# Four bias products on 32 rows each: one expert block of a streaming encoder on one Trainium2 core

## The chip, the cores and the metric

The kernel runs on one core of one Trainium2 chip. The time is device microseconds (us) of one execution, and lower is better. The engines are named as in the profile: PE is TensorE's matmuls and PEld its weight loads, DVE is VectorE, ACT is ScalarE, POOL is GpSimd, and SP is the engine that issues most of the transfers.

## The reference, cut to what matters

The block normalises its input, runs attention and a linear recurrence, projects, normalises again, and then sends each of 512 tokens through 4 of 32 experts. Only the expert part and its biases bear on this change:

```python
def expert_block(args):
    xb, e = args
    hb = xb @ w_up[e] + b_up[e]          # (128, 1024) @ (1024, 2048) + (2048,)
    glu, lin = jnp.split(hb, 2, axis=-1)
    ...
    return act @ w_down[e] + b_down[e]   # (128, 1024) @ (1024, 1024) + (1024,)
```

Everything is float32. `b_up` has 32 rows (experts) of 2048 columns.

## The kernel before

The kernel has three stretches: the mixer with the output projection, the routing, and the loop over the 32 experts. Each expert has one slot of 128 tokens. Its weights come from HBM in twelve chunks of 1 MB: eight of the up projection (128 rows by 2048 columns) and four of the down projection. Line 74 issues these loads on SP's queue whenever one of ten raw tiles (`w_raw`) is free. Each chunk is split into a high and a low part: line 87 rounds it on ACT (`w_hi_t`), line 89 subtracts on DVE (`w_lo_t`). A raw tile is free again once line 89 has read it. Every product is then three matmuls (lines 409 to 411): high by high, low by high, high by low.

The expert loop is written out in a fixed order by hand. For expert e it begins the up projection (`up_begin`), runs eight chunks of it with the transposes of the neighbouring experts in between, and then the four chunks of the down projection of expert e-1. On TensorE the last matmul of a down projection is thus followed by the bias products of the next expert, and these by its first chunk.

The bias of the up projection is added by matmul. `bias` is a tile of 128 rows by 2048 columns in bfloat16: rows 0 to 31 hold the first bfloat16 part of all 32 experts' biases, rows 32 to 63 the second part, rows 64 to 95 the third, and rows 96 to 127 zero. The stationary operand is one column of `erow_b`, broadcast to 128 columns; it is one in the three rows of expert e. Four such matmuls (line 414), one for each 512 columns, write the four PSUM tiles `ps_up_t` that the chunks then add to:

```python
    def bias_mm(self, ps, sel, j):
        self.nc.tensor.matmul(ps, sel, self.bias[:, 512 * j:512 * j + 512], start=True, stop=False)
```

Nearest to this in form is line 368 (`meta`), which runs once in four experts in the same loop: sixteen matmuls that each use 32 of the array's columns, with weights and results of 32 columns.

`prepare_up` (lines 321 to 336) fills `bias` once. It runs where the attention ends: its tiles lie in memory that the attention gives back. The bias is loaded in four pieces on ACT's queue, three casts on ACT and two subtractions on DVE form the parts, and twelve transfers on ACT's queue move each part to its rows. Around it TensorE works on the last projections of the mixer (lines 938 to 940, tile `pj`); line 1542 on ACT and line 1543 on DVE empty its two PSUM tiles. Then come the first chunks of the output weight (`w_raw` from `in_w_o`), split by lines 87 and 89. In this stretch the order on each engine comes from the compiler's scheduler, which goes by estimated times; from the normalisation behind the output projection on, the order is written by hand.

`erow` and `erow_b` are formed in `Consts` at the start. The overflow loop (line 687) serves experts with more tokens than a slot holds; in this run its body isn't entered.

Of the kernel before, what the change touches and what calls it, by code (L numbers as in the profile page):

```python
# [8 lines left out]
F32 = mybir.dt.float32  # L9
F32R = mybir.dt.float32r  # L10
BF = mybir.dt.bfloat16
I32 = mybir.dt.int32
AF = mybir.ActivationFunctionType
ALU = mybir.AluOpType
AX = mybir.AxisListType
# [6 lines left out]
NE = 32  # L22
# [9 lines left out]
BIG = 4096.0  # L32
# [10 lines left out]
class Stream:  # L43


    def __init__(self, tc):
        self.nc = tc.nc
        self.free = deque()
        self.split_ahead = 2
        self.queue = self.nc.sync  # L50
        self.src = []
        self.raws, self.parts = {}, {}
        self.loaded = self.split = 0
# [67 lines left out]
class Consts:  # L121
    def __init__(self, nc, pool, tmp):
        self.mhalf = pool.tile([128, 4], F32, name="mhalf")
        nc.gpsimd.memset(self.mhalf, -0.5)
        nc.scalar.copy(tmp.tile([128, 4], F32, name="act_table"), self.mhalf)
        jp = tmp.tile([128, 128], I32, name="jp")
        nc.gpsimd.iota(jp, pattern=[[1, 128]], base=0, channel_multiplier=-1)
        self.ident = pool.tile([128, 128], F32, name="ident")
        nc.vector.tensor_scalar(self.ident, jp, 0.0, None, op0=ALU.is_equal)
        self.before = pool.tile([128, 128], BF, name="before")  # L130
        nc.vector.tensor_scalar(self.before, jp, 0.0, None, op0=ALU.is_gt)
        self.ones = pool.tile([128, 128], BF, name="ones")
        nc.vector.memset(self.ones, 1.0)

        self.base = pool.tile([128, 1], F32, name="base")
        for b in range(NB):
            nc.gpsimd.memset(self.base[SLB * b:SLB * b + SLB, :], BIG + 128.0 * b)
        self.slots = pool.tile([128, 128], F32, name="slots")
        nc.gpsimd.iota(self.slots, pattern=[[1, 128]], base=-int(BIG), channel_multiplier=0,
                       allow_small_or_imprecise_dtypes=True)  # L140
        self.pcol = pool.tile([128, 1], F32, name="pcol")
        nc.gpsimd.iota(self.pcol, pattern=[[0, 1]], base=0, channel_multiplier=1,
                       allow_small_or_imprecise_dtypes=True)
        self.ecol = pool.tile([128, NE], F32, name="ecol")
        nc.gpsimd.iota(self.ecol, pattern=[[1, NE]], base=0, channel_multiplier=0,
                       allow_small_or_imprecise_dtypes=True)
        self.erow = pool.tile([128, NE], F32, name="erow")
        t = tmp.tile([128, NE], F32, name="sel_t")
        nc.vector.tensor_scalar(self.erow, jp[:, :NE], 0.0, None, op0=ALU.is_equal)
        for r in (1, 2):  # L150
            nc.vector.tensor_scalar(t, jp[:, :NE], -float(r * NE), None, op0=ALU.is_equal)
            nc.vector.tensor_add(self.erow, self.erow, t)
        self.erow_b = pool.tile([128, NE], BF, name="erow_b")
        nc.vector.tensor_copy(self.erow_b, self.erow)


class Moe:
# [162 lines left out]

    def prepare_up(self, tmp):

        nc = self.nc
        nc.gpsimd.memset(self.bias[96:128], 0.0)

        bq = tmp.tile([128, 512], F32, name="prep_b")
        for q in range(4):
            nc.scalar.dma_start(bq[32 * q:32 * q + 32], self.a["b_up"][0][:, 512 * q:512 * q + 512])
        for r in range(3):
            pt = tmp.tile([128, 512], BF, name=f"prep_p{r}")  # L330
            nc.scalar.copy(pt, bq)
            if r < 2:
                nc.vector.tensor_sub(bq, bq, pt)
            for q in range(4):
                nc.scalar.dma_start(self.bias[32 * r:32 * r + 32, 512 * q:512 * q + 512],
                                    pt[32 * q:32 * q + 32, :])

    def open(self, ctx, h1, h1_pool):
        tc, nc = self.tc, self.nc
# [70 lines left out]
        mm(ps, xh, wl, start=False, stop=False)  # L410
        mm(ps, xl, wh, start=False, stop=stop)  # L411

    def bias_mm(self, ps, sel, j):
        self.nc.tensor.matmul(ps, sel, self.bias[:, 512 * j:512 * j + 512], start=True, stop=False)

    def up_begin(self, sel):
        ps = [self.ps_up.tile([128, 512], F32, name="ps_up_t") for _ in range(4)]
        for j in range(4):
            self.bias_mm(ps[j], sel, j)
        return ps  # L420

    def up_chunk(self, ps, x, w, k):
# [149 lines left out]
            steps[step[0]](int(step[1]))  # L572

    def sel_of(self, e):
        return self.c.erow_b[:, e:e + 1].to_broadcast([128, 128])

    def experts(self, out):
        st = self.st
# [104 lines left out]
    def overflow(self, out):  # L683

        tc, nc, a, st = self.tc, self.nc, self.a, self.st
        n = nc.values_load(self.n_i[0:1, 0:1], min_val=0, max_val=3 * NE)
        with tc.For_i(0, n, 1) as i:
            ti = self.xp.tile([1, 2], I32, name="ov_i")
            nc.sync.dma_start(ti, self.tab_i[bass.ds(i, 1), :])
            tf = self.xp.tile([128, 2], F32, name="ov_f")  # L690
            row = self.tab_f[bass.ds(i, 1), :]
            nc.sync.dma_start(tf, row.to_broadcast([128, 2]))
            e = nc.values_load(ti[0:1, 0:1], engines=[mybir.EngineType.SP], min_val=0, max_val=NE - 1)
            em = self.xp.tile([128, NE], F32, name="ov_em")
            nc.vector.tensor_scalar(em, self.c.ecol, tf[:, 0:1], None, op0=ALU.is_equal)
            shift = self.xp.tile([128, 1], F32, name="ov_shift")
            nc.vector.tensor_scalar(shift, tf[:, 1:2], -float(SLB), None, op0=ALU.mult)
            pos = self.xp.tile([128, NB], F32, name="ov_pos")
            vals = self.xp.tile([128, NB, 5], BF, name="ov_vals")
            t = self.xp.tile([128, NE, 5], F32, name="ov_t", bufs=1)  # L700
            t3 = self.xp.tile([128, 5], F32, name="ov_t3")
            for b in range(NB):
                nc.vector.tensor_mul(t[:, :, 0], self.posm[:, b, :], em)
                nc.vector.tensor_reduce(pos[:, b:b + 1], t[:, :, 0], axis=AX.X, op=ALU.add)
                nc.vector.tensor_mul(t, self.vals[:, b], em[:, :, None].to_broadcast([128, NE, 5]))
                nc.vector.tensor_reduce(t3, t.rearrange("p e s -> p s e"), axis=AX.X, op=ALU.add)
                nc.vector.tensor_copy(vals[:, b, :], t3)
            nc.vector.tensor_scalar(pos, pos, shift, None, op0=ALU.add)
            self.onehot(pos[:, :, None], 1)
            drain(self.meta(1, lambda b, _: vals[:, b, :]))  # L710
            idx, gate = self.idx[-1], self.gate[-1]
            self.fetch(0, idx)
            drain(self.x_T(0))
            et = self.xp.tile([128, NE], F32, name="ov_et")
            nc.vector.tensor_mul(et, self.c.erow, em)
            sc = self.xp.tile([128, 1], F32, name="ov_sc")
            nc.vector.tensor_reduce(sc, et, axis=AX.X, op=ALU.add)
            sel_t = self.xp.tile([128, 1], BF, name="ov_sel")
            nc.vector.tensor_copy(sel_t, sc)
            sel = sel_t.to_broadcast([128, 128])  # L720
            wu = a["w_up"][0][bass.ds(e, 1)].rearrange("o k n -> (o k) n")
            wd = a["w_down"][0][bass.ds(e, 1)].rearrange("o k n -> (o k) n")

            def chunk(src):
                c = st.add(*src)
                return st.get(c)
            ps = self.up_begin(sel)
            for k in range(8):
                self.up_chunk(ps, self.x[0], chunk(self.up_src(wu, k)), k)
            for h in range(2):  # L730
                self.act0(ps, h)
                self.act1(ps, h)
                self.act2(h)
                drain(self.act_T(h))
            ps = self.dn_begin()
            for k in range(4):
                w = chunk(self.dn_src(wd, k))
                for kk in range(2):
                    self.dn_half(ps, w, k, kk)
            self.slots_T(idx)  # L740
            self.finish_on_chip(ps, gate, out)
# [140 lines left out]
def drain(g):  # L882
    for _ in g:
        pass
# [849 lines left out]
```

## Time and profile before

| | |
|---|---|
| median of 3 runs | 1526.08 us (1525.84 to 1527.07) |
| the profiled execution's own time | 1526.0 us |
| its span on the core | 1524.2 us |
| PE busy | 1463.3 us, 96% of the span |
| PEld busy | 1208.1 us, 79% |
| DVE busy | 1325.1 us, 87% |
| ACT busy | 1074.7 us, 71% |
| POOL busy | 263.8 us, 17% |
| HBM traffic | 310 GB/s over the span |

Busy shares are averages over stretches with different limits. Matmuls are pipelined: one that is listed with 0.39 us may start 0.23 us after the one before, so the distance between starts, and not the listed length, is what it costs. The span starts at 0 in all rows below.

### The profile page before, as it was taken

How to read it: one execution, taken by the hardware profiler on the slowest of the kernel's cores; microseconds unless marked ns; L12 is line 12 of the kernel's file. 1: busy time of each engine (PE TensorE's matmuls, PEld its weight loads, DVE VectorE, ACT ScalarE, POOL GpSimd, SP SyncE). 2: the span in 40 equal slices, each digit the busy share in tenths (PEclk: the TensorE clock that was granted, in tenths of full speed). 3: DMA queues.
4: the chain of work that ended last, by engine and by line, in shares of the span. 5: the costliest groups of instructions: out<-in, count | busy, mean ns of one | idle time of the engine just before them, and what ended most of it. 6: DMA issues, size and time to landing. Idle time of an engine off the chain costs nothing. (4 is left out here: it accounts for less than half of the span.)

```text
span 1524.2 us, 20021 instructions
## 1 busy us (share of the span) xinstructions
PE 1463.3 (96%) x7366; PEld 1208.1 (79%) x7398; DVE 1325.1 (87%) x1519; ACT 1074.7 (71%) x1149; POOL 263.8 (17%) x249
## 2 busy tenths in 40 slices
PE   7999999979999999999999999999999999999983
PEld 5878998767888888888888888888888888888863
DVE  8867877668999999999999999999999999999975
ACT  4678453347777777777777777777777777777762
POOL 5120414230111111111111111111111111111033
PEclk9999999999999999999999999999999999999997
DMA  5222145367999999999999999999999999999943
GB/s 201 86 81 56 29 147 189 145 212 288 346 366 371 374 358 374 369 377 364 366 376 356 375 361 372 359 378 371 374 359 371 374 368 370 372 366 365 362 152 119
DMA packets 100730, 457.15 MB, mean 300 GB/s; under 512 B 14032, under 2 KB 24697, under 8 KB 67859
## 3 DMA queue, kind: packets, MB, share of 16 engines
q1 hardware_dynamic: 86002, 425.51, 74.4%
q0 software_dynamic: 12672, 29.50, 6.6%
q8 instruction: 60, 0.98, 0.3%
q10 hardware_dynamic: 1952, 0.80, 0.2%
q14 instruction: 44, 0.35, 0.1%
HBM read 447.26 MB, written 24.64 MB: 310 GB/s over the span
## 5 line engine op out<-in xcount | busy, mean ns | idle before, releaser
L89 DVE TENSOR_TENSOR w_lo_t<-w_raw,w_hi_t 128x2048 fp32r<-128x2048 f32 (+1 forms) x391 | 881.3, 2274 | 87.5 <-ACT w_hi_t L87 86.8
L87 ACT CAST w_hi_t<-w_raw 128x2048 fp32r<-128x2048 f32 (+1 forms) x391 | 724.8, 1900 | 1.7 <-PE ps_up_t L411 1.2
L409 PE MATMUL ps_up_t<-w_hi_t,xh 128*128 128x512 f32 x1024 | 420.0, 410 | 0.0
L411 PE MATMUL ps_up_t<-w_hi_t,xl 128*128 128x512 f32 x1024 | 403.4, 394 | 0.0
L410 PE MATMUL ps_up_t<-w_lo_t,xh 128*128 128x512 f32 x1024 | 400.2, 391 | 0.0
L473 POOL DMA_INDIRECT acc_dram<-h,idx x31 | 97.4, 3142 | 955.1 <-ACT h L472 748.4
L411 PEld LDWEIGHTS ps_up_t<-w_hi_t,xl 128*128 128x128 f32 x1024 | 192.7, 188 | 43.6
L409 PEld LDWEIGHTS ps_up_t<-w_hi_t,xh 128*128 128x128 f32 x1024 | 193.2, 189 | 39.7 <-issue 0.8
L410 PEld LDWEIGHTS ps_up_t<-w_lo_t,xh 128*128 128x128 f32 x1024 | 193.4, 189 | 37.4
L411 PE MATMUL ps_dn_t<-w_hi_t,h 128*128 128x512 f32 x512 | 199.8, 390 | 1.1 <-DVE h L455 1.1
L409 PE MATMUL ps_dn_t<-w_hi_t,h 128*128 128x512 f32 x512 | 200.1, 391 | 0.3 <-ACT h L454 0.3
L410 PE MATMUL ps_dn_t<-w_lo_t,h 128*128 128x512 f32 x512 | 199.9, 390 | 0.0
L411 PEld LDWEIGHTS ps_dn_t<-w_hi_t,h 128*128 128x128 f32 x512 | 96.5, 189 | 21.6 <-DVE h L455 1.5
L409 PEld LDWEIGHTS ps_dn_t<-w_hi_t,h 128*128 128x128 f32 x512 | 96.6, 189 | 20.5 <-ACT h L454 0.5
L410 PEld LDWEIGHTS ps_dn_t<-w_lo_t,h 128*128 128x128 f32 x512 | 96.5, 189 | 20.1
L403 ACT CAST xh<-ps_tr 128x512 fp32r<-128x512 f32 x64 | 37.6, 588 | 88.6 <-PE ps_tr L400 88.6
L454 ACT CAST h<-ps_tr 128x512 fp32r<-128x512 f32 x64 | 37.5, 588 | 79.4 <-PE ps_tr L451 79.4
L472 ACT ACTIVATE h<-ps_dn_t,gate_s 128x512 f32<-128x512 f32 x62 | 42.4, 689 | 65.0 <-PE ps_dn_t L411 65.0
L938 PE MATMUL pj<-mw_hi,hT 128*128 128x256 f32 (+1 forms) x192 | 60.2, 314 | 2.8 <-ACT hT L1059 1.7
L939 PE MATMUL pj<-mw_lo,hT 128*128 128x256 f32 (+1 forms) x192 | 58.4, 305 | 1.1 <-DVE mw_lo L866 1.1
L940 PE MATMUL pj<-mw_hi,hT 128*128 128x256 f32 (+1 forms) x192 | 58.2, 303 | 1.3 <-DVE hT L1061 1.3
L433 ACT ACTIVATE act_l<-ps_up_t 128x512 f32<-128x512 f32 x64 | 38.4, 601 | 23.7 <-PE ps_up_t L411 23.7
(363 smaller groups left out, 1803.3 us busy)
## 6 DMA issues: line engine op xcount, KB each, us to landing
w_raw<-in_w_up SPq DMA_DIRECT2D x256, 1024.0 KB
w_raw<-in_w_down SPq DMA_DIRECT2D x128, 1024.0 KB
mw_raw<-in_w_in SPq DMA_DIRECT2D x16, 512.0 KB
w_raw<-in_w_o SPq DMA_DIRECT2D x4, 1024.0 KB
mw_raw<-in_w_in SPq DMA_DIRECT2D x4, 672.0 KB
h_dram<-x POOLq DMA_DIRECT2D x4, 512.0 KB, 3.5
h<-h_dram POOLq DMA_DIRECT2D x4, 512.0 KB, 5.2
rows_dram<-h POOLq DMA_DIRECT2D x4, 512.0 KB, 4.7
```

Source lines behind the costliest of these rows:

```text
L87: self.nc.scalar.copy(h[:, s], r[:, s])
L89: self.nc.vector.tensor_sub(l[:, s], r[:, s], h[:, s].bitcast(F32))
L403: nc.scalar.copy(xh[:, s, :], p)
L409: mm(ps, xh, wh, start=start, stop=False)
L410: mm(ps, xh, wl, start=False, stop=False)
L411: mm(ps, xl, wh, start=False, stop=stop)
L433: nc.scalar.activation(self.l_bufs[h], ps[2 + h], AF.Copy, bias=1.0)
L472: nc.scalar.mul(y[:, 512 * n:512 * n + 512], ps[n], gate)
L473: nc.gpsimd.indirect_dma_start(out=self.acc[:, :], out_offset=bass.IndirectOffsetOnAxis(ap=idx[:, :1], axis=0), in_=y, in_offset=None, bou ...
L938: mm(ps, xh, wh, start=start, stop=False, skip_group_check=True)
L939: mm(ps, xh, wl, start=False, stop=False, skip_group_check=True)
L940: mm(ps, xl, wh, start=False, stop=stop, skip_group_check=True)
```

## The change

The four bias products of an expert become four matmuls that each contract over 32 rows: product j uses rows 32j to 32j+31 of both operands. For that `bias` has another layout. In rows 32j to 32j+31 lie the biases of output columns 512j to 512j+511: three bfloat16 parts of eight rows each (expert e modulo 8), and the tile's four column blocks hold the four groups of eight experts (e // 8). The last eight rows of each 32 are zero. `erow_b` has ones where a row's number modulo 8 and its part fit the expert.

`prepare_up` now clears a float32 tile of 128 x 2048 on POOL, loads the bias into it in twelve transfers on POOL's queue (each part's rows get the same values), and forms the parts in place: after each cast on ACT, DVE subtracts the cast value from the rows of the later parts (`later` is -1 there and 0 elsewhere). The third cast writes `bias` itself, so the twelve transfers to `bias` are gone. The rows that `erow` needs are formed here too, by fourteen small operations on DVE, in place of six in `Consts`. The overflow loop's body changes likewise (sixteen products in place of four); it isn't entered.

```diff
 class Consts:
-        t = tmp.tile([128, NE], F32, name="sel_t")
-        nc.vector.tensor_scalar(self.erow, jp[:, :NE], 0.0, None, op0=ALU.is_equal)
-        for r in (1, 2):
-            nc.vector.tensor_scalar(t, jp[:, :NE], -float(r * NE), None, op0=ALU.is_equal)
-            nc.vector.tensor_add(self.erow, self.erow, t)
         self.erow_b = pool.tile([128, NE], BF, name="erow_b")
-        nc.vector.tensor_copy(self.erow_b, self.erow)
...
     def prepare_up(self, tmp):
-        nc = self.nc
-        nc.gpsimd.memset(self.bias[96:128], 0.0)
-
-        bq = tmp.tile([128, 512], F32, name="prep_b")
-        for q in range(4):
-            nc.scalar.dma_start(bq[32 * q:32 * q + 32], self.a["b_up"][0][:, 512 * q:512 * q + 512])
+        nc, c = self.nc, self.c
+        b = tmp.tile([128, 2048], F32, name="prep_b")
+        nc.gpsimd.memset(b, 0.0)
         for r in range(3):
-            pt = tmp.tile([128, 512], BF, name=f"prep_p{r}")
-            nc.scalar.copy(pt, bq)
+            for j in range(4):
+                p = 32 * j + 8 * r
+                nc.gpsimd.dma_start(b[p:p + 8, :].rearrange("i (g n) -> i g n", g=4),
+                                    self.a["b_up"][0][:, 512 * j:512 * j + 512].rearrange("(g i) n -> i g n", g=4))
+
+        row = tmp.tile([128, 32], F32, name="prep_row")
+        t = tmp.tile([128, 32], F32, name="prep_t")
+        for j in range(4):
+            nc.vector.tensor_scalar(t if j else row, c.slots[:, 0:32], BIG + 32.0 * j, c.pcol,
+                                    op0=ALU.add, op1=ALU.is_equal)
+            if j:
+                nc.vector.tensor_add(row, row, t)
+        later = tmp.tile([128, 2], F32, name="prep_later")
+        for r in range(2):
+            nc.vector.tensor_reduce(later[:, r:r + 1], row[:, 8 * r + 8:24], axis=AX.X, op=ALU.add)
+        nc.vector.tensor_scalar(later, later, -1.0, None, op0=ALU.mult)
+        nc.vector.tensor_add(t[:, 0:8], row[:, 0:8], row[:, 8:16])
+        nc.vector.tensor_add(t[:, 0:8], t[:, 0:8], row[:, 16:24])
+        for x in (c.erow, c.erow_b):
+            nc.vector.tensor_copy(x.rearrange("p (g i) -> p g i", g=4), t[:, None, 0:8].to_broadcast([128, 4, 8]))
+
+        for r in range(3):
+            pt = tmp.tile([128, 2048], BF, name="prep_p") if r < 2 else self.bias
+            nc.scalar.copy(pt, b)
             if r < 2:
-                nc.vector.tensor_sub(bq, bq, pt)
-            for q in range(4):
-                nc.scalar.dma_start(self.bias[32 * r:32 * r + 32, 512 * q:512 * q + 512],
-                                    pt[32 * q:32 * q + 32, :])
+                nc.vector.scalar_tensor_tensor(b, pt, later[:, r:r + 1], b, op0=ALU.mult, op1=ALU.add)
...
-    def bias_mm(self, ps, sel, j):
-        self.nc.tensor.matmul(ps, sel, self.bias[:, 512 * j:512 * j + 512], start=True, stop=False)
-
-    def up_begin(self, sel):
+    def up_begin(self, sels):
+
         ps = [self.ps_up.tile([128, 512], F32, name="ps_up_t") for _ in range(4)]
-        for j in range(4):
-            self.bias_mm(ps[j], sel, j)
+        for i, (sel, g) in enumerate(sels):
+            for j in range(4):
+                p = slice(32 * j, 32 * j + 32)
+                self.nc.tensor.matmul(ps[j], sel[p], self.bias[p, 512 * g:512 * g + 512], start=i == 0, stop=False)
         return ps
...
     def sel_of(self, e):
-        return self.c.erow_b[:, e:e + 1].to_broadcast([128, 128])
+        return [(self.c.erow_b[:, e:e + 1].to_broadcast([128, 128]), e // 8)]
```

## Rows read from the trace of the kernel before

**Rows 1.** Busy time by stretch: length, PE, PEld, DVE, ACT, POOL, PEclk, DMA share, GB/s.
```profile
220.00:230.00 10.00, 9.62 (x79) 9.28 (x77) 4.58 (x7) 4.79 (x8) 1.40 (x2) 1.00 1.01 374
...
405.00:1440.00 1035.00, 1032.95 (x4831) 839.77 (x4859) 953.49 (x672) 800.41 (x640) 131.63 (x57) 1.00 0.99 368
```

**Rows 2.** What PE waited for, 345 to 1440: total, times, longest us.
```profile
PE ps_up_t L414 <- DVE h L438: 1.8, 2, 1.6
PE ps_up_t L414 <- ACT act_l L433: 1.2, 2, 0.6
```

**Rows 3.** Costliest groups, 600 to 900: count, busy us, mean ns, idle before.
```profile
L89 DVE TENSOR_TENSOR w_lo_t<-w_raw,w_hi_t 128x2048 fp32r<-128x2048 f32 x102 | 231.4, 2288 | 22.7 <-ACT w_hi_t L87 22.5
L87 ACT CAST w_hi_t<-w_raw 128x2048 fp32r<-128x2048 f32 x102 | 190.5, 1914 | 0.0
```

**Rows 4.** What SP's queue waited for, 400 to 1440.
```profile
SPq L74 <- DVE w_lo_t L89: 720.8, 284, 3.6
```

**Rows 5.** Line 414: count, min/median/max ns, first and last start.
```profile
L414 PEld LDWEIGHTS <-erow_b x128: 95/98/152, 338.5 to 1439.7; 128*128 128x128 bf16 x128
```

**Rows 6.** PE in order of time around one bias block: start, us.
```profile
832.64 0.39 PE L411 MATMUL ps_dn_t<-w_hi_t,h 128*128 128x512 f32 x1
...
833.32 0.39 PE L411 MATMUL ps_dn_t<-w_hi_t,h 128*128 128x512 f32 x1
833.78 0.81 PE L414 MATMUL ps_up_t<-bias,erow_b 128*128 128x512 bf16 x3
...
834.65 0.39 PE L410 MATMUL ps_up_t<-w_lo_t,xh 128*128 128x512 f32 x1
```

**Rows 7.** PE in order of time around line 368.
```profile
819.30 0.39 PE L411 MATMUL ps_up_t<-w_hi_t,xl 128*128 128x512 f32 x1
819.62 0.27 PE L368 MATMUL ps_tr<-vals,oh 128*32 128x5 bf16 x16
...
820.15 0.40 PE L410 MATMUL ps_up_t<-w_lo_t,xh 128*128 128x512 f32 x1
```

**Rows 8.** Line 368: count, min/median/max ns, first and last start.
```profile
L368 PE MATMUL ps_tr<-vals,oh x144: 163/166/180, 330.6 to 1247.7; 128*32 128x5 bf16 x112, 128*32 128x2 bf16 x16, 128*32 128x3 bf16 x16
```

**Rows 9.** The instructions of prepare_up: count, min/median/max ns, first and last start.
```profile
L328 ACTq DMA_DIRECT2D prep_b<-in_b_up x4: 384/418/445, 221.0 to 222.3; - x4
L331 ACT CAST prep_p<-prep_b x3: 618/619/619, 229.1 to 235.8; 128x512 bf16<-128x512 f32 x3
L333 DVE TENSOR_TENSOR prep_b<-prep_b,prep_p x2: 693/694/694, 229.7 to 233.3; 128x512 f32<-128x512 f32 x2
...
L335 ACTq DMA_DIRECT2D bias<-prep_p x12: 514/596/645, 229.7 to 238.3; - x12
```

**Rows 10.** POOL in order of time, 150 to 345.
```profile
220.87 0.52 POOL L1242 MEMSET hsc<- 128x512 f32 x1
236.99 1.04 POOL L118 TENSOR_TENSOR h_rs<-rsq_t,mhalf 128x4 f32<-128x4 f32 x1 [15.59 <-DVE rsq_t L117]
...
243.00 2.22 POOL L1578 DMA_DIRECT2D h<-h_dram  x4 [0.98 <-PE pj L940]
```

**Rows 11.** DVE in order of time: at the start, and where the output weights are split.
```profile
7.21 0.19 DVE L152 TENSOR_TENSOR erow<-erow,sel_t 128x32 f32<-128x32 f32 x1
...
245.91 5.14 DVE L89 TENSOR_TENSOR w_lo_t<-w_raw,w_hi_t 128x2048 fp32r<-128x2048 f32 x2
```

**Rows 12.** Waits between 218 and 250: of ACT, then of PE.
```profile
ACT prep_p L331 <- DMA prep_b<-in_b_up: 3.1, 1, 3.1
...
PE pj L938 <- DVE gs L1543: 1.1, 2, 0.7
```

**Rows 13.** PE in order of time at the first output products.
```profile
251.10 0.50 PE L939 MATMUL pj<-w_lo_t,cat 128*128 128x512 f32 x1 [0.28 <-DVE w_lo_t L89]
```

**Rows 14.** Line 1700, the first reader of the bias tile.
```profile
L1700 PE MATMUL warm<-bias,ones x17: 376/379/379, 315.7 to 330.2; 128*128 128x512 bf16 x17
```

More of the change, by code (lines that the diff above doesn't have):

```diff
@@ L715, in overflow @@
             nc.vector.tensor_mul(et, self.c.erow, em)
-            sc = self.xp.tile([128, 1], F32, name="ov_sc")
-            nc.vector.tensor_reduce(sc, et, axis=AX.X, op=ALU.add)
-            sel_t = self.xp.tile([128, 1], BF, name="ov_sel")
+            sc = self.xp.tile([128, 4], F32, name="ov_sc")
+            nc.vector.tensor_reduce(sc, et.rearrange("p (g i) -> p g i", g=4), axis=AX.X, op=ALU.add)
+            sel_t = self.xp.tile([128, 4], BF, name="ov_sel")
             nc.vector.tensor_copy(sel_t, sc)
-            sel = sel_t.to_broadcast([128, 128])
+            sel = [(sel_t[:, g:g + 1].to_broadcast([128, 128]), g) for g in range(4)]
             wu = a["w_up"][0][bass.ds(e, 1)].rearrange("o k n -> (o k) n")
```

## The prediction

> **What bounds the kernel now.** I read the busy time by stretch first [rows 1]. In the expert loop PE is busy 1032.95 of 1035 us, at a granted clock of 1.00, which is the upper of its two levels, 2.4 GHz. DVE is busy for 92% (953.49 of 1035), and the DMA engines for 99% at 368 GB/s. Three resources are near full, so busy shares can't say which of them sets the pace; the waits can. From 345 on PE waited for other engines for 3.0 us in all [rows 2]. The casts of the raw weights on ACT waited for nothing, no load among it, and the subtractions on DVE waited for ACT's casts [rows 3]. SP's loads waited 720.8 us for line 89 to free a raw tile [rows 4]. So the loads run ahead until the tiles are full, and PE is what the others wait for. A shorter PE program per expert should shorten the loop, until DVE or the loads become the bound.
>
> **What four products cost now.** The loop has 128 of them, four in each of 32 experts [rows 5]. In [rows 6] the matmuls of a product start 0.227 us apart (832.64 to 833.32, three steps). From the last one of the down projection (833.32) to the second one of the up projection (834.65) is 1.33 us. Two steps of 0.227 would pass without the bias, so the block adds 0.88 us. One product streams for 0.215 us: three matmuls cover 0.81, of which the last is 0.38, which leaves 0.43 for two steps. Four make 0.86, and 0.02 is lost at the edges.
>
> **What four products on 32 rows each would cost.** No matmul of this trace runs beside others on other rows. The nearest is line 368: sixteen matmuls on groups of 32 columns, between the same neighbours [rows 7]. From 819.30 to 820.15 is 0.85 us; less two steps, the block adds 0.40 us. The sixteen cover 0.27 us and the last is listed with 0.17 [rows 7, 8], so they all start within 0.10 us, 6 ns apart: matmuls on different parts of the array do overlap. The other 0.30 us passes before the first and behind the last: 0.09 between the end of the stream before (819.30 + 0.227) and 819.62, and 0.21 behind the last start, until the weights of the next product are in. A bias block has no such edges (0.02).
>
> I take these edges for the new form too, since it also divides the array: 0.30 us, plus one stream of 0.215, plus three starts of 6 ns, less a little for what the last small matmul streams itself (one step of 6 ns up to 0.02 us). That makes 0.52 us in place of 0.88, so 0.36 us less for each expert and 32 x 0.36 = **11.5 us** less in the loop. The bounds lie far apart. If rows need no such edges, the block takes 0.215 + 0.02 + 0.02 = 0.25, and 32 x 0.63 = 20 us are saved. If each edge waits for a whole matmul to leave the array, that is 0.39 listed less 0.215 streamed, 0.175 twice, with 0.19 for a weight load (the same listing gives 0.21 behind line 368, which holds both): 0.215 + 0.02 + 0.35 + 0.19 = 0.78, and 3 us are saved.
>
> The edges of line 368 belong to columns, and the sum rests on carrying them over to rows. The Trainium skill says in TensorEngine Tiling (Array Packing), Key Properties, that changing the tiling mode, and not only the tile, drains the engine; that would hold for rows as well. The trace agrees for columns; no run here shows it for rows yet. By that rule the sum is the one above; without it the bound of 20 us would be the sum.
>
> **What hides behind this gain.** DVE needs 953.49/1035 of the time now and 93% of a loop that is 1% shorter (0.36 of 35.6 us per expert), so it stays below PE. The loads would have to rise by the same 1%, from 368 to 372 GB/s; between 220 and 230 they reached 374 [rows 1]. Even at no more than 368 they don't bind at once: ten raw tiles of 1 MB are 28 us of loading, and as the casts never wait, some of them are full. Half of these, 14 us, cover the 11.5 us that PE gains over the loop.
>
> **The preparation.** It comes at 221 us, 95 us before the tile's first reader at 315.7 [rows 14], so the bias itself can't be late. What can matter is who stands behind it on ACT, DVE and POOL, while PE is busy 9.62 of 10 us [rows 1] and needs line 1543 to empty its two PSUM tiles.
> Removed: sixteen issues on ACT (4 x 0.42 + 12 x 0.60 = 8.8 us), three casts of 0.62 and two subtractions of 0.69 [rows 9]. ACT's wait of 3.1 us for the bias lay in front of line 1542, and PE then waited 1.1 us for line 1543 [rows 12].
> Added on POOL: a clear of 128x2048, four times the 0.52 of 128x512, or 2.1 us, and twelve issues of 0.55 (2.22 for four), 6.6 us. POOL is idle for 15.6 us there, so they end at about 230, before line 118 needs POOL at 237 [rows 10]. The old load landed 6.8 us behind its last issue (222.3 to 229.1 [rows 9]); with 4 to 6 us the new one lands at 234 to 236.
> Added on ACT: three casts of 1.91 (line 87's mean for this size [rows 3]), 3.9 us more than before, less the 8.8 of issues. Added on DVE: two steps of 2.29 in place of 0.69, and fourteen small operations of about 0.19 (2.7 us; the six removed at the start were 1.1) [rows 3, 11].
> The chain is 3 x 1.91 + 2 x 2.29 = 10.3 us and so ends at 244 to 246, just where the output weights are split: line 89 works on them from 245.91, and PE waits 0.28 us for it at 251.10 [rows 11, 13]. There is no room left at that point. If everything fits into idle time, 1.1 us is gained. If ACT takes the first cast too early, it waits until 235 in place of 229, 6 us more, and with a cast and a subtraction in front of the split (1.9 + 2.3) the loss is 10 us. I take 1.5 us of loss, near the low end: of 20 us from 220 to 240 DVE and ACT are idle for about half, and the old chain cost PE 1.1 us. Removed work at the start costs nothing: the six operations fill DVE's idle time there.
>
> **The sum.** The profiled execution took 1526.0 us (span 1524.2, 1.8 around it), the median of the runs is 1526.08. 1526.0 - 11.5 + 1.5 = **1516 us**.
>
> **The rivals.**
> *No edges for rows:* the block takes 0.25 us. For it: weights of 128 rows load in the background now, with edges of 0.02 [rows 6]. Against: line 368. 1526 - 20 + 1.5 = 1507.5 us. TensorE: Matmul & The Clock Gate of the Trainium skill, Part 3, gives 3.07 times for four products on 32 rows and 512 columns; an estimate from that is 0.86/3.07 = 0.28 us, close to this case. No row of this trace shows it.
> *Longer edges, or part of the gain given back to DVE or the loads:* 3 to 8 us saved, 1519 to 1524.5 us.
> *The preparation stalls PE by 5 to 10 us:* 1519.5 to 1524.5 us. For it: nothing is free at 245 to 251. Against: 10 us of idle time before.
> *The four don't overlap, slower:* the rows' streams go one behind the other, and the edges come on top. 0.86 + 0.30 + 0.02 = 1.18 us, 0.30 more for each expert, 9.6 us: 1526 + 9.6 + 1.5 = 1537 us. It decides from the point where the block exceeds 0.88 less the preparation's 0.05 per expert: 0.83 - 0.32 = 0.51 of streams, so at 2.4 streams in place of one. Against it: the 6 ns of line 368, though its results are five columns and go to one PSUM tile, where here 512 columns go to four.
>
> **Numbers.** Forecast 0.57 (1512 to 1519), no edges 0.13, longer edges or given back 0.14, preparation 0.09, no overlap 0.07. Without no overlap, the last of the others and a little of no edges, 1506 to 1523 holds eight in ten. A measurement here tells about 0.2% or 3 us: faster is below 1523.0, slower above 1529.1. Faster: 0.57 + 0.13 + most of the other two (0.13) = 0.83; same 0.10; slower 0.07.
>
> **What the profile will show.** By the forecast the four matmuls of line 414's successor start within 0.03 us; from the matmul before the block to the second one behind it there is 0.97 us in place of 1.33; successive experts lie 0.36 us closer; ACT's casts still wait for no load, and PE's clock stays at 1.00. Four starts 0.215 apart would show no overlap, a block of 0.25 no edges. PE's waits on DVE or casts that wait for loads would show a new bound. Between 220 and 255, PE's idle time shows the preparation's cost. The forecast is wrong above all if the edges of rows aren't those of columns.

## The result: 0.8% slower, and the profile after

The changed kernel took 1539.37 us (median of 4 runs, 1536.09 to 1541.75) against 1525.96 for the kernel before beside it. The ratio is 1.0083, with a 95% interval of 1.0067 to 1.0100. The forecast was 1516 us, faster.

The loop did what was forecast. The weight loads of the bias products, line 430 now (count, min/median/max ns, first and last start), answer to [rows 5]:

```profile
L430 PEld LDWEIGHTS <-erow_b x128: 89/91/102, 363.7 to 1454.2; 32*128 32x128 bf16 x128
```

The loop from first to last lasts 1454.2 - 363.7 = 1090.5 us; before it was 1439.7 - 338.5 = 1101.2 [rows 5]. So 10.7 us are gained there, but it starts 25.2 us later. What is behind it takes 85.7 us of the span of 1539.9, 1.2 more than before. The profiled execution's own time is the sum: 1526.0 + 25.2 - 10.7 + 1.2 = 1541.7 us. It lies 2.4 us above the median. By the ratio the change costs 12.7 us, and so the loop starts some 22 us later (12.7 + 10.7 - 1.2). And 1.5 of the 25.2 us are there before the preparation begins: ACT's last copy of the attention to `a_u` runs at 218.06 (line 1403), and before at 216.57 (line 1392).

PE in order of time around one block answers to [rows 6]:

```profile
853.78 0.39 PE L422 MATMUL ps_dn_t<-w_hi_t,h 128*128 128x512 f32 x1
854.10 0.40 PE L430 MATMUL ps_up_t<-bias,erow_b 32*128 32x512 bf16 x4
854.43 0.50 PE L420 MATMUL ps_up_t<-w_hi_t,xh 128*128 128x512 f32 x1
854.77 0.40 PE L421 MATMUL ps_up_t<-w_lo_t,xh 128*128 128x512 f32 x1
```

The four products are listed with 0.40 together, hardly more than one, so they start within some 0.02 us. From the matmul before the block to the second one behind it is 0.99 us in place of 1.33, and the block adds 0.53 where 0.52 was forecast. The edges are those of line 368: 0.09 us lie between the end of the stream before (853.78 + 0.227) and 854.10. The Trainium skill says in TensorEngine Tiling (Array Packing), Key Properties, that a change of tiling mode drains the engine; for rows, too, the trace now agrees.

From 405 on PE waits for no other engine, and the casts of line 87 wait for no load. Nearly the whole loss lies in front of the loop. Busy time by stretch, 215 to 300, as in [rows 1], of the kernel after:

```profile
215.00:230.00 15.00, 12.21 (x95) 11.87 (x94) 11.93 (x35) 6.66 (x24) 10.70 (x15) 0.91 0.88 320
230.00:245.00 15.00, 15.00 (x112) 15.00 (x111) 3.81 (x10) 2.87 (x8) 2.84 (x6) 0.86 0.54 50
245.00:260.00 15.00, 9.47 (x66) 8.90 (x64) 11.06 (x12) 9.75 (x7) 8.44 (x7) 0.82 0.70 256
260.00:275.00 15.00, 11.68 (x52) 10.69 (x51) 12.33 (x17) 6.36 (x6) 5.13 (x5) 0.50 0.40 165
275.00:300.00 25.00, 25.00 (x142) 21.91 (x141) 13.96 (x27) 0.86 (x2) 5.25 (x8) 0.93 0.00 1
```

And of the kernel that I call fours below, which has the same loop and whose steps up to 290 us, where I compared them, lie within 0.2 us of those of the kernel before:

```profile
215.00:230.00 15.00, 14.62 (x123) 14.23 (x121) 8.70 (x17) 6.47 (x15) 4.10 (x6) 1.00 0.91 327
230.00:245.00 15.00, 14.29 (x121) 14.26 (x120) 8.73 (x26) 8.61 (x24) 4.11 (x6) 1.00 0.14 38
245.00:260.00 15.00, 14.70 (x94) 12.79 (x93) 14.85 (x16) 5.11 (x3) 9.49 (x7) 1.00 0.94 341
260.00:275.00 15.00, 14.98 (x102) 13.38 (x102) 12.19 (x24) 0.96 (x2) 6.80 (x10) 1.00 0.22 71
275.00:300.00 25.00, 24.25 (x131) 20.43 (x130) 16.23 (x36) 10.79 (x26) 3.64 (x5) 1.00 0.40 146
```

Two things are to be seen. PE has gaps (9.47 of 15 us busy). And its granted clock falls to 0.50, the lower of the two levels, so that from 260 to 275 it is busy for 11.68 us with 52 matmuls, where fours does 102 in 14.98. Over the five stretches it runs 467 matmuls in place of 571.

The two longest waits of PE between 215 and 300 (total, times, longest us):

```profile
PE hg L1282 <- DVE hsc L1272: 3.9, 1, 3.9
PE pj L949 <- DVE gs L1554: 2.8, 1, 2.8
```

Both waits are for DVE. In order of time, the 2.8 us first. DVE's rows, then POOL's:

```profile
222.47 1.87 DVE L330 TENSOR_SCALAR prep_row<-slots,pcol 128x32 f32<-128x32 f32 x1 [1.20 <-POOL sq L1414]
222.62 1.74 DVE L330 TENSOR_SCALAR prep_t<-slots,pcol 128x32 f32<-128x32 f32 x1
...
227.19 0.25 DVE L341 CAST erow_b<-prep_t 128x32 bf16<-128x32 f32 x1
227.48 0.42 DVE L1554 TENSOR_TENSOR gs<-gs,pj 128x256 f32<-128x256 f32 x1
...
250.64 4.47 DVE L89 TENSOR_TENSOR w_lo_t<-w_raw,w_hi_t 128x2048 fp32r<-128x2048 f32 x2
255.03 0.71 DVE L1272 COPY_PREDICATED hsc<-masks,hg 128x512 f32<-128x512 uint8 x1
```

```profile
222.49 1.81 POOL L320 MEMSET prep_b<- 128x2048 f32 x1
...
226.21 4.45 POOL L324 DMA_DIRECT2D prep_b<-in_b_up  x8
233.47 0.55 POOL L324 DMA_DIRECT2D prep_b<-in_b_up  x1 [2.82 <-DMA prep_b<-in_b_up]
...
235.78 0.54 POOL L324 DMA_DIRECT2D prep_b<-in_b_up  x1 [0.17 <-issue]
```

The fourteen small operations of `prepare_up` stand from 222.47 to 227.4 in front of line 1554, which takes the gates `gs` and so frees a PSUM tile for PE. Two of them take 1.87 and 1.74 us while POOL clears `prep_b`. They overlap, and both end at 224.3, where the clear ends; another of the same kind took 0.24. PE stood for 2.8 us. Its granted clock fell at 227.3, while it stood, and was at the lower level until 234.1. The Trainium skill says in SBUF — State Buffer, section "SBUF: two separate sides", that VectorE and GpSimd share one pair of ports, which an operation of GpSimd, or one of VectorE in a two-port mode, holds for its whole length while the other is blocked. The two rows fit that; none shows the mode.

Then ACT, in order of time:

```profile
248.50 7.29 ACT L87 CAST w_hi_t<-w_raw 128x2048 fp32r<-128x2048 f32 x4
255.69 1.90 ACT L345 CAST prep_p<-prep_b 128x2048 bf16<-128x2048 f32 x1
264.46 1.90 ACT L345 CAST prep_p<-prep_b 128x2048 bf16<-128x2048 f32 x1 [6.88 <-DVE prep_b L347]
268.78 1.90 ACT L345 CAST bias<-prep_b 128x2048 bf16<-128x2048 f32 x1 [2.42 <-DVE prep_b L347]
270.71 2.56 ACT L1419 ACTIVATE cat<-at,cols 128x512 fp32r<-128x512 f32 x4
```

Line 1419 (`attn_out`, line 1408 before) writes `cat`, the input of the out projection. In the kernel before it ran from 224.0. Here it comes last, behind the four casts of the output weights and the three of the preparation. So the out products, long and dense, begin at 275.74 in place of 246. First two lines of before, then two of after:

```profile
223.98 1.94 ACT L1408 ACTIVATE cat<-at,cols 128x512 fp32r<-128x512 f32 x3
246.10 0.72 PE L938 MATMUL pj<-w_hi_t,cat 128*128 128x512 f32 x2
```

```profile
255.80 1.54 PE L1282 MATMUL hg<-QF,KG 128*128 128x64 f32 x6 [3.85 <-DVE hsc L1272]
...
275.74 0.77 PE L949 MATMUL pj<-w_hi_t,cat 128*128 128x512 f32 x1
```

Until then PE has only the recurrence, short matmuls with a DVE step between them. In the 3.85 us in which it stood, at 254.6, the clock fell to its lower level, and it stayed there until 278.5.

Why `cat` is late I could read from the addresses of the built program, which no trace holds: the scratch of `prepare_up` (its temporary tiles) ended at byte 95744 of a partition before and ends at 103200 now, and `cat0`, the first buffer of `cat`, begins at 98272. So `cat0` has to wait until the scratch is free. The run pad, below, shows the same by an edit.

### The profile page after: what moved, and what is told of

It is laid out like the page before. It is cut to its first block, busy times and chain, and to the rows that moved or that the text cites. A ratio compares the mean times of both kernels' runs of the same rounds, so it can differ in the third digit from the quotient of the medians.

```text
span 1539.9 us, 20060 instructions
## 1 busy us (share of the span) xinstructions
PE 1471.4 (96%) x7396; PEld 1213.9 (79%) x7398; DVE 1331.7 (86%) x1527; ACT 1078.5 (70%) x1149; POOL 268.6 (17%) x261
```

## The experiments

**Theory A**: that overlap with `cat0` is the loss. **Theory B**: the work of the new preparation is, by what it stands in front of on ACT, DVE and POOL. **Theory C**: the 32-row products have a part in it. Each ratio is to runs of the kernel before on the same chip. "Starts" is the first and "lasts" the time from the first to the last weight load of the bias products, in one profiled execution.

| kernel | median us | ratio, 95% interval | loop starts | lasts |
|---|---|---|---|---|
| before | 1526.08 | 1 | 338.5 | 1101.2 |
| after | 1539.37 | 1.0083 (1.0067 to 1.0100) | 363.7 | 1090.5 |
| no_prep | 1526.42 | 1.0000 (0.9991 to 1.0010) | 338.1 | 1101.6 |
| loop_alone | 1515.75 | 0.9925 (0.9908 to 0.9942) | 339.0 | 1090.3 |
| prep_alone | 1549.12 | 1.0147 (1.0129 to 1.0165) | 357.2 | 1101.5 |
| stride | 1519.43 | 0.9947 (0.9933 to 0.9961) | 344.2 | 1090.2 |
| pad | 1522.31 | 0.9958 (0.9943 to 0.9973) | 342.6 | 1091.3 |
| **fours** | 1517.17 | 0.9935 (0.9922 to 0.9948) | 337.9 | 1090.5 |
| ops | 1516.29 | 0.9926 (0.9902 to 0.9949) | 339.1 | 1090.4 |
| mid_free | 1523.78 | 0.9987 (0.9975 to 1.0000) | 346.2 | 1090.7 |
| mid_over | 1526.42 | 0.9998 (0.9984 to 1.0012) | 348.2 | 1090.0 |
| wide | 1526.37 | 1.0001 (0.9991 to 1.0011) | 350.5 | 1090.5 |
| fit | 1537.55 | 1.0072 (1.0055 to 1.0089) | 359.1 | 1089.8 |
| early | 1542.59 | 1.0102 (1.0084 to 1.0120) | 355.8 | 1100.4 |
| early64 | 1546.41 | 1.0131 (1.0114 to 1.0148) | 354.7 | 1101.3 |
| halves | 1546.90 | 1.0124 (1.0104 to 1.0145) | 359.5 | 1100.6 |
| halves_act | 1535.81 | 1.0057 (1.0042 to 1.0073) | 348.5 | 1100.3 |
| nudge | 1526.36 | 0.9998 (0.9987 to 1.0008) | 338.7 | 1100.1 |
| align | 1525.99 | 0.9995 (0.9986 to 1.0005) | 338.6 | 1100.1 |
| nudge128 | 1524.47 | 0.9977 (0.9967 to 0.9986) | 340.2 | 1098.9 |

### The two parts of the change by themselves

**no_prep**, the kernel before with an empty preparation, which leaves out the biases:

```diff
     def prepare_up(self, tmp):
-        bq = tmp.tile([128, 512], F32, name="prep_b")
-        ...
+        self.nc.gpsimd.memset(self.bias, 0.0)
```

> The kernel before without its preparation: prepare_up only clears the bias tile, so the up projection's biases are left out, and the four products of 128 rows stay as they were. It prices the old preparation. Theory A (the loss of the change is a wait on memory that its larger scratch brings): the old scratch had no such wait, so without it the time stays within 6 us of before, 1520 to 1527 us. Theory B (the preparation's ACT and DVE work is itself in TensorE's way at 220 to 260 us): the old one was a fourth of the size and still cost some of it, so 1512 to 1519 us.

The old preparation costs nothing that the times show: ratio 1.0000. **loop_alone** is the same with the new products:

> The kernel after with four 32-row products in each expert, and no preparation at all: the bias tile is cleared and the selection columns are formed as before, so the biases of the up projection are left out. Beside no_prep it prices the loop alone. Theories A and B: 10.7 us under no_prep, the step from the first expert's first weight load to the last's being 1090.5 us as in the kernel after. Theory C (the row products themselves bring the loss, by what they leave for the stages around them): level with no_prep or above it.

It was 1515.75, 10.7 us under no_prep, and the loop lasts 1090.3 us. The products bring the whole gain and none of the loss; Theory C falls. **prep_alone** has the new preparation and the old products:

```diff
-                self.nc.tensor.matmul(ps[j], sel[p], self.bias[p, 512 * g:512 * g + 512], start=i == 0, stop=False)
+            self.nc.tensor.matmul(ps[j], sels[0][0], self.bias[:, 512 * j:512 * j + 512], start=True, stop=False)
```

> The preparation of the kernel after with the four 128-row products of the kernel before, which then add the biases of other experts to the up projection. Theories A and B: the loss before the loop stays whole and the loop's gain is gone, 1526 + 25 = 1551 us, the loop starting near 364 us. Theory C (the row products have a part in the loss in front of the loop): under 1545 us.

1549.12, 22.9 us over before, with the loop as long as before (1101.5). The start is at 357.2, not 364: most of the loss, and some 6 us apart from it, by an edit that is in the loop alone. The order isn't the reason: up to the loop PE, ACT, DVE and POOL run the same instructions in the same order in both traces (but for two warm-up matmuls of line 1700 that only one trace lists). Of the 6.5 us, 1.7 are there ahead of the preparation (`a_u` at 216.37 in place of 218.06). The rest goes with the clock. PE stood for 2.5 us here, in place of 2.8, and its clock didn't fall. The stretch behind that wait, first in after, then in prep_alone:

```profile
227.30:234.10 6.80, 6.15 (x29) 6.15 (x29) 1.88 (x7) 0.38 (x1) 3.90 (x8) 0.50 1.13 224
225.00:232.00 7.00, 6.00 (x50) 6.00 (x51) 3.68 (x14) 1.71 (x5) 4.66 (x10) 1.00 1.11 245
```

From 100 us to the loop's start the clock was at the lower level for 40.8 us in after and for 30.2 in prep_alone. The profiled execution of after took 2.4 us more than its median, that of prep_alone 3.1 us less. So starts of the loop, read from one execution each, can differ by some 6 us with no difference in the program in front of it.

### The overlap, tried on the kernel after

**fit** moves `cat0` out of the way with fewer staging tiles for the output weights:

```diff
-RAW_A = 4
+RAW_A = 3
...
-RAW_B = 4
+RAW_B = 5
```

> The kernel after with one staging buffer of w_o fewer (three in place of four, and one more in the later set), so that the output tile cat0 no longer shares memory with the preparation's scratch; every instruction of the preparation stays. Theory A: attn_out comes before the preparation's casts again, the first of them near 224 us, the out projection's products begin near 247 us, and the time falls to 1514 to 1522 us (the loop's 10.7 us less, the 2.8 us wait for the small DVE operations and the low clock behind it kept). Theory B: the casts and operations still stand in the way and the time stays at 1533 to 1541 us.

`attn_out` came early, as expected, at 220.8 us, but the time was 1537.55. The edit brought a loss of its own. The fourth output weight now came late, DVE's line 1618 stood behind its split and the preparation's first subtraction, and PE waited 7.9 us for that (its wait, then ACT's row):

```profile
PE pj L949 <- DVE h L1618: 7.9, 1, 7.9
258.84 1.90 ACT L87 CAST w_hi_t<-w_raw 128x2048 fp32r<-128x2048 f32 x1 [6.81 <-DMA w_raw<-in_w_o]
```

So fit decides nothing. **halves** makes the scratch fit in another way:

```diff
-        b = tmp.tile([128, 2048], F32, name="prep_b")
+        b = tmp.tile([128, 1024], F32, name="prep_b")
         nc.gpsimd.memset(b, 0.0)
+        for h in range(2):
+            ...
+            pt = self.bias[:, 1024 * h:1024 * h + 1024]
```

> The kernel after with the preparation in two halves of 1024 columns: scratch of 4 KB a partition, the casts written straight into the bias tile, the small DVE operations moved to the constants at the start; all parts are computed. No tile shares its memory with cat0. Theory A: the whole loss goes, 1512 to 1518 us. Theory B (the work itself): the same casts and operations, so 1530 us or more; only the small operations' 2 to 3 us go.

1546.90, a miss for A. The second half's loads waited on POOL for the first half's last cast, and the second run of line 1295 of the recurrence stood behind them; in the kernel before (line 1284) it ran at 248.9:

```profile
256.31 6.77 POOL L341 DMA_DIRECT2D prep_b<-in_b_up  x12 [5.85 <-ACT bias L345]
263.11 2.61 POOL L1295 TENSOR_TENSOR KG<-KG,f 128x256 f32<-128x256 f32 x1
```

**halves_act** only puts the 24 loads on another queue:

```diff
-                    nc.gpsimd.dma_start(b[p:p + 8, :].rearrange("i (g n) -> i g n", g=2),
+                    nc.scalar.dma_start(b[p:p + 8, :].rearrange("i (g n) -> i g n", g=2),
```

> As halves, with the 24 loads on ACT's queue in place of POOL's. In halves twelve loads held POOL from 256.3 to 263.1 us in front of L1295's products, and the time was 1546.9 us. Theory E (the place in an in-order queue decides: POOL's products come late, TensorE is left with gaps and the low clock): 1514 to 1525 us, if ACT has room for the issues. Theory B (casts and DVE work): 1535 us or more.

The loop starts at 348.5 in place of 359.5, and the ratios differ by 10 us: so much lay in the queue, with what else moved by the new order on the engines. The time, 1535.81, lies in B's range all the same, because its loop lasts 1100.3 us, 9.8 more than the same products need in fours. halves has that too. The cause is in the last group.

### The old preparation with the new products

**stride** keeps the old short preparation and reaches a 32-row layout by its stores:

```diff
+            for g in range(4):
+                nc.scalar.dma_start(self.bias[r::4, 512 * g:512 * g + 512], pt[32 * g:32 * g + 32, :])
```

> The four 32-row products of the kernel after, with the preparation of the kernel before: 512-column casts, 5 KB of scratch a partition, four loads and twelve stores on ACT's queue. The stores reach the new layout because row 4*(8*j+i)+r now holds part r of chunk j, so that a store writes every fourth partition; the selection is formed once, at the start. All parts are computed. Theory A and Theory B (the loss is the new preparation's, by a wait on memory or by its work in front of others in the queues): 1513 to 1518 us, level with loop_alone. Theory C (the row products do it when real biases are prepared): 1530 us or more.

0.9947, some 8 us faster than before, 1.4 us above the range. The first cast stood on ACT in front of the gates and waited for the loads until 231.90 (229.1 before [rows 9]):

```profile
231.90 0.62 ACT L332 CAST prep_p<-prep_b 128x512 bf16<-128x512 f32 x1 [5.31 <-DMA prep_b<-in_b_up]
```

**pad** adds nothing but the overlap:

```diff
-            pt = tmp.tile([128, 512], BF, name=f"prep_p{r}")
+            pt = tmp.tile([128, 2048], BF, name=f"prep_p{r}")[:, 0:512]
```

> As stride, with the three cast tiles of the scratch allocated four times as wide (a fourth of each is used), so that the scratch ends at 104960 and shares memory with cat0 again; no instruction is added. Theory A (the overlap alone is the loss): attn_out waits for the preparation's end near 240 us, and the time is 5 us or more over stride. Theory B (the work): cat0 is in time for the first out product near 247 us anyway, and the time is within 2 us of stride.

`attn_out` moved from 224.7 to 244.6, but the loop started no later (342.6 against 344.2), and the intervals of the times overlap. With a short preparation the overlap costs nothing. **fours** deals the experts to the column groups by e mod 4, so that loads and stores both have one stride:

```diff
-                                self.a["b_up"][0][8 * g:8 * g + 8, :].rearrange("i (j n) -> j i n", j=4))
+            nc.scalar.dma_start(bq[32 * q:32 * q + 32], self.a["b_up"][0][:, 512 * q:512 * q + 512])
...
-                nc.scalar.dma_start(self.bias[r::4, 512 * g:512 * g + 512], pt[32 * g:32 * g + 32, :])
+                nc.scalar.dma_start(self.bias[r::4, 512 * g:512 * g + 512], pt[g::4, :])
```

> As stride, with the experts dealt to the column groups by e mod 4 in place of e div 8, so that the four loads are again those of the kernel before (in stride two loads took ACT's queue 1.99 and 1.30 us in place of 0.87 and 0.86, the first cast came at 231.9 us, and TensorE waited 4.1 us for gates that stood behind it). Theory F (what is left of the loss in stride, 5.3 us at the loop's start, is those loads): the first cast comes near 229 us, the loop starts within 1.5 us of loop_alone's, and the ratio to before is that of loop_alone, 0.992 to 0.994, 1515 to 1517 us. Rival: the row-strided stores hold ACT, and nothing changes against stride (0.9947).

The first cast came at 228.99, the loop starts at 337.9, and the ratio is 0.9935, within the interval of loop_alone. It computes all that the kernel before does, is 9.0 us under it, and by the ratios (1.0083 and 0.9935) 22.6 us under the kernel after: the version to keep. **ops** issues the fourteen small operations in it:

```diff
+        for j in range(4):
+            nc.vector.tensor_scalar(t if j else row, c.slots[:, 0:32], BIG + 32.0 * j, c.pcol,
+                                    op0=ALU.add, op1=ALU.is_equal)
+            ...
```

> As fours, with the fourteen small DVE operations of the kernel after issued in prepare_up as there, into tiles that nobody reads. If they cost by themselves: the gates behind them come late, TensorE waits about 2.8 us, its clock falls, and the loop starts 5 to 9 us later than in fours, 1522 to 1526 us. Rival (only beside the long preparation): within 2 us of fours.

They cost nothing here (0.9926). The first took 0.47 us beside POOL's shorter clear of another tile, and again it ended where the clear ended, at 221.6 to 221.7:

```profile
221.20 0.47 DVE L333 TENSOR_SCALAR prep_row<-slots,pcol 128x32 f32<-128x32 f32 x1 [1.20 <-POOL sq L1419]
221.11 0.52 POOL L1258 MEMSET hsc<- 128x512 f32 x1
```

### What in the new preparation

**wide** is fours with the new preparation's widths, the clear on POOL, and one cast tile in place of three, so that a cast has to wait until the stores have read the one before:

```diff
-        bq = tmp.tile([128, 512], F32, name="prep_b")
+        b = tmp.tile([128, 2048], F32, name="prep_b")
+        nc.gpsimd.memset(b, 0.0)
+        bq = b[:, 0:512]
...
-            pt = tmp.tile([128, 512], BF, name=f"prep_p{r}")
+            pt = tmp.tile([128, 2048], BF, name="prep_p")
```

> As fours, with the scratch of the kernel after: an 8 KB tile that POOL clears, three casts and two subtractions over 2048 columns (a fourth of them used), overlap with cat0; the loads and stores stay those of fours, and the small operations stay out. Theory B (the wide casts and subtractions and what they push back): 6 us or more over fours. Rival (loads and their queue are what costs): within 3 us of fours.

The gain of 9 us is gone (1.0001); the loop starts 12.6 us later than in fours. PE waited here:

```profile
PE pj L939 <- ACT cat L1409: 4.4, 1, 4.4
PE pj L939 <- ACT mw_hi L865: 3.2, 1, 3.2
```

**mid_free** and **mid_over** are built like wide, hold the work at 1272 columns and differ from each other in the overlap alone:

```diff
-            pt = tmp.tile([128, 1272], BF, name="prep_p")
+            pt = tmp.tile([128, 2400], BF, name="prep_p")[:, 0:1272]
```

> As fours, with casts and subtractions over 1272 columns in place of 512 (512 are used) and a scratch cleared by POOL that just ends in front of cat0: more work, no overlap. Theory B (the work): half of wide's 9 us or more over fours, 1520 us up. Theory A (the overlap, once the preparation ends late): within 2 us of fours.

> As mid_free, instruction for instruction, with the cast tile allocated 2400 columns wide, so that the scratch reaches into cat0. Theory A: 4 us or more over mid_free, cat0's first product behind the third cast. Theory B: within 2 us of mid_free.

Without the overlap the wider casts and subtractions, with the clear and the single cast tile, cost 8.3 us at the loop's start, and of the 0.65% that fours gains 0.13% are left. With it 2.0 us come on top, and between 215 and 300 PE's longest wait is now for `cat` (3.1 us); `attn_out` itself waited 3.2 us there for the stores out of the scratch, which the kernel after doesn't have. Counted from `a_u` (218.2 and 216.0), ahead of the preparation, the two steps are 6.6 and 4.1 us. The times, 0.9987 and 0.9998, have intervals that overlap. So Theory B holds for the greater part, and A's part is 2 to 4 us in these traces and not shown by the times. What the overlap costs beside the whole new preparation no run shows: fit and halves take it away, but each brings a loss of its own.

**early** takes the small operations out of the kernel after:

```diff
 class Consts:
+        later = self.later = pool.tile([128, 2], F32, name="later")
+        ...
     def prepare_up(self, tmp):
-        later = tmp.tile([128, 2], F32, name="prep_later")
-        ...
```

> The kernel after with the fourteen small DVE operations of prepare_up moved to the constants at the start; scratch, loads, casts and the overlap with cat0 stay. Theories A and B: the 2.8 us wait at 225 us and the half clock behind it go, 1532 to 1537 us. Theory D (the small operations in front of the gates start the whole loss by way of the clock): 1522 us or less.

The loop starts 7.9 us earlier (355.8) than in the profiled execution of after, more than expected, and yet the time was 1542.59, since the loop lasts 1100.4 us. **early64** adds 32 unused bytes to it:

> As early, with 32 unused bytes more, so that the tiles behind move by 64 bytes in place of 32. Theory G: the loop has the 1090 us of the kernel after again and the time is 1532 to 1535 us, 9 us under early, which leaves 5 to 8 us of the loss to the small DVE operations. Rival (early's longer loop had another reason): 1541 us or more.

A miss: the start stays early (354.7), but the loop is as long as in early.

### A move by 32 bytes

early, halves and halves_act hold one small tile more among the constants, so the tiles behind it lie 32 bytes further. **nudge** is fours with such a tile, unused:

```diff
+        pool.tile([128, 8], F32, name="nudge")
         self.erow_b = pool.tile([128, NE], BF, name="erow_b")
```

> As fours, with an unused tile of 32 bytes a partition in front of erow_b, so that the tiles behind it (bias, xh, xl, xg among them) move by 32 bytes; no instruction is added. In early, halves and halves_act, which hold such a tile, an expert took 35.53 us in place of 35.20 with the same bias block, and the up products followed each other in 3.3 ns more. Theory G (the address does it): the loop is 10 us longer than in fours, the time 1525 to 1527 us. Rival (the selection in the constants or the preparation does it): level with fours.

9.2 us over fours; the whole gain is lost without one more instruction. The groups of PE between 650 and 1250 us, first fours, then nudge (count, busy us, mean ns):

```profile
L410 PE MATMUL ps_up_t<-w_hi_t,xl 128*128 128x512 f32 x544 | 213.6, 393 | 0.0
L409 PE MATMUL ps_up_t<-w_lo_t,xh 128*128 128x512 f32 x544 | 212.5, 391 | 0.0
```

```profile
L411 PE MATMUL ps_up_t<-w_hi_t,xl 128*128 128x512 f32 x544 | 215.2, 396 | 0.0
L410 PE MATMUL ps_up_t<-w_lo_t,xh 128*128 128x512 f32 x544 | 214.8, 395 | 0.0
```

Each of these products takes 3 to 4 ns more; an expert takes 35.54 us in place of 35.23. **align** moves the weights' tiles instead:

```diff
+    rp("w_shift", 1).tile([128, 8], F32, name="w_shift")
     st.grow([rp(f"w_raw_a{i}", 1) for i in range(RAW_A)])
```

> As fours, with an unused tile of 32 bytes above the weights' buffers, so that w_raw, w_hi and w_lo move by 32 bytes while xh and xl stay. If the place of the moving weights against the stationary tiles counts, the loop is about 10 us longer, as in nudge; if the address of xh and xl alone counts, it is level with fours.

The ratio is 0.9995, as for nudge. With early64, which moves the stationary tiles by 64 bytes, this speaks against their address modulo 64 and fits the distance between them and the weights. **nudge128** moves by 128 bytes (`[128, 32]` in place of `[128, 8]`):

> As fours, with 128 unused bytes a partition in front of erow_b. If the distance from xh and xl to the weights' tiles modulo 128 bytes decides (it is a multiple of 128 in every kernel so far with a short loop, 64 or 96 over one in every kernel with a long one): level with fours. If any move from the distance of the kernel before costs: 9 us over fours, as in nudge.

0.9977, by the ratios 6 us over fours, so a distance that is a multiple of 128 doesn't suffice. In the built programs (no trace holds their addresses) the short loop goes with 88064 bytes from `xh` to `w_hi`, in fit too, where both lie elsewhere; the long one with 88032 (nudge, align, early and both halves), 88000 (early64) and 87936 (nudge128). Whether it is the distance, and what about it, is open.

## Why the prediction was wrong

- **The loop's gain** held: 10.7 us against 11.5, the block 0.53 against 0.52. The edges of line 368 carried over to rows, and the rivals of the loop (no edges, longer edges, no overlap) fell. The 3.07 times (TensorE: Matmul & The Clock Gate of the Trainium skill, Part 3) don't hold for this block: with its edges it shrank 0.88/0.53 = 1.66 times.
- **The preparation's price** is the step that failed: "I take 1.5 us of loss, near the low end", with 10 us as the bound. It was 25 us in the profiled execution and some 22 by the ratio. The rival of a stall was right in kind and had 5 to 10 us and a chance of 0.09. The time, 1539.37, lies next to the 1537 of the rival in which the four products don't overlap; that is chance, since they do.
- The sum priced each instruction and laid it into idle time. Its chain of 10.3 us was to end at 244 to 246; it ended at 270.7. The loads' issues were to end at 230 and ended at 236.3: they began at 226.2, and the last four waited for earlier ones to land. The first cast, expected from 235 on, came at 255.69, put behind the output weights' casts.
- "There is no room left at that point" named the place, but not who is late next: `attn_out` on ACT, line 1272 and the gates on DVE. Nor did the sum hold the price of a gap in clock: the matmuls behind the gaps ran at 0.50 for 24 us (254.6 to 278.5), and for 7 us at 227.3. The clock "stays at 1.00" only from 398 on.
- How the 25.8 us between fours and after divide, as one path through the starts of the loop: casts and subtractions of 1272 columns, with the clear and the single cast tile, 8.3; the overlap 2.0; the full width 2.3; twelve loads on POOL's queue with `attn_out` last 4.2 (wide to early64); the small operations 9.0 (early64 to after). These starts are of one execution each. Counted from `a_u`, ahead of the preparation, the steps are 6.6, 4.1, 0.2, 6.1 and 7.1. Nor is the last one the price of the small operations: prep_alone has them too, in the same order, and lies only 2.3 us behind early64 by this count. The rest is the clock of that execution of after. By the ratios, less what the loops differ by, early lies 7 us under after and early64 3.5. So they cost between 2 and 7 us here, and nothing in fours; none of these is a price that adds up elsewhere. For the other steps it stays open how much is the order that the build chose.

## What to carry to other kernels

A stage like this one, which weaves two streams on engines that take their work in a fixed order, can have no idle time to give away, however the busy shares look: price a longer setup by who stands behind it on each queue, and by what TensorE has left to do meanwhile. Change the layout with the strides of transfers that are there already before doing more arithmetic for it. And when an edit only adds or moves a tile, compare the addresses of TensorE's operands too, before its instructions are blamed. Compare starts in two traces only after looking where the two executions already differ ahead of the change, and at which clock they ran.

## What was unexpected of the hardware

Moving the stationary tiles by 32, 64 or 128 bytes a partition, or the weights by 32, made the loop 8.4 to 10.8 us longer (1098.9 to 1101.3 against 1090.5 us), 3 to 4 ns for each product of 128 x 512 in the up projection; those of the down projection stayed at 389 to 390 ns. DVE operations of the same kind on 32 columns took 0.23 to 0.26 us with no clear on POOL beside them, and 0.34 to 2.33 us beside one: in after, prep_alone, fit and ops each that ran into a clear ended 0.03 to 0.06 us behind its end.
